# The order of the seven products, and of their loads, in the tokens-stationary groups of a hybrid decoder trunk

## The chip, the core and the metric

The kernel runs on one core of one Trainium2 chip. A core has five engines with a queue each: TensorE (PE in the profile; its weight loads are listed apart as PEld), VectorE (DVE), ScalarE (ACT), GpSimd (POOL) and SyncE (SP). SP and POOL also issue DMA transfers between the chip's main memory and SBUF. TensorE writes into PSUM, of which this kernel uses eight banks of 128 × 512 float32; VectorE and ScalarE read them out. The metric is the device time of one execution in microseconds (us), as a median over runs, lower is better.

## The reference

Two layers of a decoder trunk on 512 tokens of width 1024, all in float32. Each layer has one wide input projection that feeds a dilated-window attention and a chunked retention, two projections that are merged by sigmoid gates, an output projection and a SwiGLU feed-forward part. What matters here is the input projection:

```python
z = jnp.einsum('bsd,dc->bsc', x, w_in) + b_in
q_a, k_a, v_a, q_r, k_r, v_r, g_r, gate_a, gate_b = jnp.split(z, SPLIT_POINTS, axis=-1)
...
y_r = _retention(q_r, k_r, v_r)                       # reshapes left out
y_b = (jax.nn.silu(g_r) * y_r.reshape(B, S, RET_V_WIDTH)).astype(x.dtype)
```

`v_a` (the attention's values, 1152 columns), `v_r` and `g_r` (the retention's values and its gate, 2048 columns each, in four heads of 512) are the columns that the changed groups compute.

## The kernel before

**Precision.** Each float32 matrix is split into a high and a low part (`hi` is a cast by ScalarE, `lo` a subtraction by VectorE), and a product is the sum of three matmuls: high × high, high × low and low × high.

**Seven products in place of eight.** A group computes a 2 × 2 block product. The left side is x transposed, cut into token halves and halves of the depth: A11, A12, A21, A22, and four sums of them, S1 to S4, that are made once per sublayer (tiles `xh`, `xl` for the blocks, `xs` for the sums). The right side is a block of weights, B11, B12, B21, B22: the first index is the half of the depth, the second is one of two column ranges. Four sums of weights stand beside them: P1, P2, P3 and P4. The seven products are M1 = A11·B11, M2 = A12·B21, M3 = S4·B22, M4 = A22·P4, M5 = S1·P1, M6 = S2·P2 and M7 = S3·P3. Three chains accumulate in PSUM (`CHAIN`, L296): chain A takes M1, M6, M7 and M4 on top of each other and is read out in between after each of them, chain X is M2 alone, and chain C takes M5 and then M3.

**Two kinds of groups.** In a *tokens-stationary* group (`tall`, L372) x is loaded into the PE array and the weights stream by; each product is done for two token tiles (`a` = 0, 1), 24 matmuls in all, and has two PSUM banks per chain. In a *wide* group (`wide`, L393) the weights are loaded into the array and x streams. The tokens-stationary groups are, per layer: two groups of 288 columns for the attention's values (the loop over `t` that calls `biased`; one bias row enters as an extra matmul from tile `bh` before each half of M1 and M5), and four groups of 512 columns, one per retention head (`ret_values_gates`). That makes 12 groups in two layers. Each head's group follows that head's `rotary`, the projection of its queries and keys; between the matmuls, `tick` feeds in *side work* from a list, such as score blocks of the retention, at a set pace.

**The weights of a group** (class `Right`, L301). `load` issues, name by name and in two units of half the depth each, a DMA from SP into a `raw` tile (pool `rawp`, eight tiles for the whole kernel). For P1 and P3 the tile first takes one block (B11 or B12) and then a second DMA, issued by POOL, adds another block to it in flight (L316, B12 or B22). P2 is made from P1 by a VectorE addition of B22 in place (L342), P4 from P2 by an addition of B21. `high` casts a unit on ScalarE (`whi`, L325), `low` subtracts on VectorE (`wlo`, L331); `whi` and `wlo` have four tiles each, so the units of two products. `operands` (L345) casts one product ahead. A raw tile comes free when its last cast and subtraction (or addition) is done, and the next load, often that of the next group, takes it.

**Read-outs** (`ev` in `biased`, L451). After M1, M5 and M6 ScalarE copies the bank to a work tile (`sn`, L453; the pool `wk` has six tiles). After M2 VectorE adds it to the copy of M1; after M7 it subtracts from the copy of M5 (L460); the result for M3 is subtracted from with the copy of M6 (L457); M4 is read directly. The value groups write the results to main memory (`v_d`) by SP's DMAs (L762).

**What sets the order.** The code is a straight line; a tile library makes the semaphores and, before the run, chooses the order of each queue, which need not be that of the code. Products are written in the order of the tuple `ORDER` (L294): M1, M2, M5, M3, M6, M7, M4. As M3 comes before M6 there and its read-out needs M6's copy, `tall` does that read-out after M6. Loads are written in the order B11, B21, P1, P3, B22.

Of the kernel before, what the change touches and what calls it, by code (L numbers as in the profile page):

```python
# [18 lines left out]
P = 128  # L19
# [34 lines left out]
def hybrid_kernel(ctx, tc, x, rel_bias, w_in, b_in, w_attn_proj, w_ret_proj, w_out,  # L54
# [25 lines left out]
    def mm(ps, a, b, start, stop):  # L80
        pe.matmul(ps, lhsT=a, rhs=b, start=start, stop=stop, skip_group_check=True)  # L81

    def mm3(ps, ah, al, bh, bl, start, stop):
        mm(ps, ah, bh, start, False)
        mm(ps, ah, bl, False, False)
        mm(ps, al, bh, False, stop)

    def psum(name="px"):
        return psm.tile([P, S], F32, tag="mm", name=name)

    def hilo(src, hi, lo):
        act.copy(out=hi, in_=src)  # L92
        dve.tensor_tensor(out=lo, in0=src, in1=hi.bitcast(F32), op=ALU.subtract)  # L93
# [4 lines left out]
    def work(name):  # L98
        return wk.tile([P, S], F32, tag="w2", name=name)

    def rows(w):
        return w.rearrange("(k p) c -> p k c", p=P)
# [30 lines left out]
    def tick(us):  # L133

        if side:
            credit[0] += rate[0] * us
            while side and credit[0] >= 1.0:
                credit[0] -= 1.0
                side.popleft()()
# [138 lines left out]
    def tail_units(raws):  # L278

        out_ = []  # L280
        for j, r in enumerate(raws):
# [12 lines left out]
    ORDER = ((1, "A11", "B11"), (2, "A12", "B21"), (5, "S1", "P1"), (3, "S4", "B22"),  # L294
             (6, "S2", "P2"), (7, "S3", "P3"), (4, "A22", "P4"))
    CHAIN = {1: "A", 6: "A", 7: "A", 4: "A", 2: "X", 5: "C", 3: "C"}  # L296
    FIRST = (1, 2, 5)
    WIDE = tuple(ORDER[i] for i in (0, 2, 4, 1, 5, 3, 6))
    WIDE1 = tuple(ORDER[i] for i in (0, 1, 2, 4, 3, 5, 6))

    class Right:  # L301

        def __init__(self, src, shapes, order=ORDER, loads=("B11", "B21", "P1", "P3", "B22")):
            self.src, self.shapes, self.order, self.loads, self.t = src, shapes, order, loads, {}

        def load(self, *names):
# [41 lines left out]
                ahead = self.begin(self.order[i + 1][2]) if i + 1 < len(self.order) else None  # L351
                yield now

    def pair_right(w1, w2, c, order=WIDE):

        def src(b, u):
            k = 4 if b[1] == "2" else 0
            return (w2 if b[2] == "2" else w1)[:, k:k + 4, c:c + 256]

        return Right(src, [(4, 256)], order, ("B11", "P1", "B22", "P3", "B21"))  # L360
# [11 lines left out]
    def tall(right, n, left, ev, bias_=None):  # L372


        ps = {}
        for (i, an, bn), units in zip(ORDER, right.operands()):
            ks = [(u, k) for u in units for k in range(u[0].shape[1])]
            c = CHAIN[i]
            for a in range(2):
                fresh = i in FIRST  # L380
                if fresh:
                    ps[c, a] = psum("ps")[:, :n]
                if bias_ is not None and i in (1, 5):
                    mm(ps[c, a], ones, bias_[:, (i != 1) * n:(i != 1) * n + n], True, False)
                    fresh = False
                ts_ = slice(a * P, (a + 1) * P)
                for j, ((h, l), k) in enumerate(ks):
                    p_ = ps[c, a]
                    ah, al = left(an, j, ts_)
                    mm(p_, ah, h[:, k], fresh and j == 0, False)  # L390
                    mm(p_, ah, l[:, k], False, False)
                    mm(p_, al, h[:, k], False, j == len(ks) - 1)
                    tick(STEP * n / 512)  # L393
                if i != 3:
                    ev(i, a, ps[c, a])
                if i == 6:
                    ev(3, a, ps["C", a])
            yield

    def wide(right, left, ev):  # L400


        ps = {}
        for (i, an, bn), ((h, l),) in zip(right.order, right.operands()):
            c = CHAIN[i]
            if i in FIRST:
                ps[c] = psum("ps")
            for q in range(2):
                cs = slice(q * P, (q + 1) * P)
                for k in range(4):  # L410
                    ah, al = left(an, k, slice(0, 256))
                    mm3(ps[c][:, q * 256:(q + 1) * 256], h[:, k, cs], l[:, k, cs], ah, al,
                        i in FIRST and q == 0 and k == 0, k == 3)
                    tick(STEP / 2)
            ev(i, ps[c])
# [29 lines left out]
    def biased(right, n, rows_, left, right_done):  # L445


        sn = {}

        def ev(i, a, ps):  # L450
            if i in (1, 5, 6):  # L451
                sn[i, a] = work("sn")[:, :n]
                act.copy(out=sn[i, a], in_=ps)  # L453
            elif i == 2:
                left(a, ps, sn[1, a])
            elif i == 3:
                dve.tensor_tensor(out=sn[6, a], in0=ps, in1=sn[6, a], op=ALU.subtract)  # L457
                right_done(a, sn[6, a])
            elif i == 7:
                dve.tensor_tensor(out=sn[5, a], in0=sn[5, a], in1=ps, op=ALU.subtract)  # L460
                right_done(2 + a, sn[5, a])
            elif i == 4:
                left(2 + a, ps, None)

        return tall(right, n, x_left, ev, rows_)
# [158 lines left out]
    def layer(ly, cp):  # L624
# [197 lines left out]
        with stage("ret") as rp:  # L822
# [85 lines left out]
            def gates(dp, sa, sb):  # L908

                sn = {}  # L910

                def put(o_, v, c, ts_):
                    for q in range(2):
                        act.activation(out=o_[:, q, ts_], in_=v[:, q], func=AF.Sigmoid, bias=bcol(c + (2 * dp + q) * P))

                def ev(i, ps):
                    p2 = ps.rearrange("p (q t) -> p q t", q=2)
                    if i in (1, 5, 6):
                        sn[i] = work("sn").rearrange("p (q t) -> p q t", q=2)
                        act.copy(out=sn[i], in_=p2)  # L920
                    elif i == 2:
                        dve.tensor_tensor(out=sn[1], in0=p2, in1=sn[1], op=ALU.add)
                        put(sa, sn[1], C_GA, slice(0, 256))
                    elif i == 3:
                        dve.tensor_tensor(out=sn[6], in0=p2, in1=sn[6], op=ALU.subtract)
                        put(sb, sn[6], C_GB, slice(0, 256))
                    elif i == 7:
                        dve.tensor_tensor(out=sn[5], in0=sn[5], in1=p2, op=ALU.subtract)
                        put(sb, sn[5], C_GB, slice(256, 512))
                    elif i == 4:  # L930
                        put(sa, p2, C_GA, slice(256, 512))

                wide(pair_right(w_l[:, :, C_GA:], w_l[:, :, C_GB:], dp * 256), x_left, ev)
                act.dma_start(g_d[1, dp * 256:(dp + 1) * 256].rearrange("(e p) s -> p e s", p=P), sb)
# [17 lines left out]
            for dp in range(KD // 2):  # L952
# [6 lines left out]
                for e in range(2):  # L959
                    cs = slice(e * P, (e + 1) * P)  # L960
                    ps = psum("ps")
# [93 lines left out]
        wg_l, wu_l, wd_l = rows(w_ffn_gate[ly]), rows(w_ffn_up[ly]), rows(w_ffn_down[ly])  # L1055
# [16 lines left out]
        def ffn_pair(f, o_):  # L1072

            sn = {}

            def put(v, ts_):
                hilo(v, o_[:, 0, :, ts_], o_[:, 1, :, ts_])

            def ev(i, ps):
                p2 = ps.rearrange("p (q t) -> p q t", q=2)  # L1080
                if i in (1, 5, 6):
                    sn[i] = work("sn").rearrange("p (q t) -> p q t", q=2)
                    act.copy(out=sn[i], in_=p2)
                elif i == 2:
                    dve.tensor_tensor(out=sn[1], in0=p2, in1=sn[1], op=ALU.add)
                elif i == 3:
                    v = sn[6]
                    dve.tensor_tensor(out=v, in0=p2, in1=v, op=ALU.subtract)
                    act.activation(out=v, in_=v, func=AF.Silu)
                    dve.tensor_tensor(out=v, in0=v, in1=sn[1], op=ALU.mult)  # L1090
                    put(v, slice(0, 256))
                elif i == 7:
                    dve.tensor_tensor(out=sn[5], in0=sn[5], in1=p2, op=ALU.subtract)
                    act.activation(out=sn[5], in_=sn[5], func=AF.Silu)
                elif i == 4:
                    v = sn[5]
                    dve.tensor_tensor(out=v, in0=v, in1=p2, op=ALU.mult)
                    put(v, slice(256, 512))

            wide(pair_right(wu_l, wg_l, f * P, WIDE1 if f == 2 else WIDE), x_left, ev)  # L1100

        for part, (f0, f1) in enumerate(FPARTS):
            ht = []
# [89 lines left out]
```

## Time and profile before

| | us |
|---|---|
| median of 3 runs | 2190.7 |
| lowest, highest | 2188.38, 2191.09 |
| the profiled execution | 2188.09 |
| its span in the profile | 2186.3 |

The profile is that of one execution. Its span goes from the first instruction to the last and is 1.8 us shorter than the time of that execution; the rest lies around it. The page gives for each engine the time in which it was busy. Views of the trace that are used below: the *waits* (who waited for whom, in total), the *timeline* (instructions in order of time; in brackets the idle time before one and what ended it), the *windows* (busy time of each engine in a stretch), and the *DMA* view (transfers by the line that issues them, with the time to landing). Matmuls are pipelined, so their lengths overlap; the distance between two starts tells the pace.

### The profile page before, as it was taken

How to read it: one execution, taken by the hardware profiler on the slowest of the kernel's cores; microseconds unless marked ns; L12 is line 12 of the kernel's file. 1: busy time of each engine (PE TensorE's matmuls, PEld its weight loads, DVE VectorE, ACT ScalarE, POOL GpSimd, SP SyncE). 2: the span in 40 equal slices, each digit the busy share in tenths (PEclk: the TensorE clock that was granted, in tenths of full speed). 3: DMA queues.
4: the chain of work that ended last, by engine and by line, in shares of the span. 5: the costliest groups of instructions: out<-in, count | busy, mean ns of one | idle time of the engine just before them, and what ended most of it. 6: DMA issues, size and time to landing. Idle time of an engine off the chain costs nothing.

```text
span 2186.3 us, 32588 instructions
## 1 busy us (share of the span) xinstructions
PE 2160.0 (99%) x12906; PEld 1900.6 (87%) x12906; DVE 1412.5 (65%) x2035; ACT 988.1 (45%) x1597; POOL 254.1 (12%) x296
## 2 busy tenths in 40 slices
PE   8999999999999999999999999999999999999998
PEld 7977888889988899989898778888899889999996
DVE  5643677877655685747676446777777447766575
ACT  4444544545733263525245445445566233444350
POOL 3110011011000100000030100111110001000001
PEclk9999999999999999999999999999999999999999
DMA  8944266458685356656369342665577762666561
GB/s 228 244 125 104 58 165 159 132 136 192 192 307 189 91 150 133 172 134 156 95 158 260 90 92 74 152 180 144 137 191 223 267 194 58 172 150 165 123 163 39
DMA packets 305978, 338.60 MB, mean 155 GB/s; under 512 B 22862, under 2 KB 244194, under 8 KB 305697
## 3 DMA queue, kind: packets, MB, share of 16 engines
q1 hardware_dynamic: 227712, 248.81, 37.8%
q0 software_dynamic: 50832, 74.90, 18.2%
q10 hardware_dynamic: 27280, 12.80, 2.0%
q8 instruction: 101, 1.65, 0.3%
q14 instruction: 53, 0.43, 0.1%
HBM read 310.67 MB, written 28.53 MB: 155 GB/s over the span
## 4 chain that ended last, share of the span: by engine, by line
PE 82%; issue 9%; DMA 3%; DVE 3%; ACT 1%; POOL 1%; POOLq 0%; DVEq 0%; ACTq 0%; SPq 0%
PE ps L81 75%; PE px L81 5%; DMA raw<-in_w_in 2%; PE px L865 1%; PE px L533 1%; POOL ry L124 0%; DMA exd<-wb 0%; DVE wlo L331 0%; PE px L169 0%; DMA exd<-pk 0%; DVE wlo L93 0%; DVE xtok L988 0%; DMA mb<-exd 0%; DMA rb<-in_b_in 0%; ACT whi L92 0%
## 5 line engine op out<-in xcount | busy, mean ns | idle before, releaser
L331 DVE TENSOR_TENSOR wlo<-raw,whi 128x1024 fp32r<-128x1024 f32 (+1 forms) x364 | 418.1, 1150 | 210.0 <-ACT whi L325 207.3
L81 PE MATMUL ps<-xh,whi 128*128 128x256 f32 (+1 forms) x1536 | 515.7, 337 | 4.4 <-ACT whi L92 3.3
L325 ACT CAST whi<-raw 128x1024 fp32r<-128x1024 f32 (+1 forms) x364 | 358.8, 990 | 342.1 <-PE ps L81 198.5
L81 PE MATMUL ps<-xh,wlo 128*128 128x256 f32 (+1 forms) x1536 | 500.5, 327 | 1.1 <-DVE wlo L93 0.9
L81 PE MATMUL ps<-xl,whi 128*128 128x256 f32 (+1 forms) x1536 | 500.5, 326 | 0.2 <-DVE xl L93 0.2
L81 PE MATMUL ps<-xs,whi 128*128 128x256 f32 (+1 forms) x2048 | 404.6, 296 | 0.0
L81 PEld LDWEIGHTS ps<-xs,whi 128*128 128x128 f32 x2048 | 327.8, 191 | 10.3
L93 DVE TENSOR_TENSOR wlo<-raw,whi 128x1024 fp32r<-128x1024 f32 (+2 forms) x162 | 193.3, 1195 | 200.9 <-ACT whi L92 200.5
L81 PEld LDWEIGHTS ps<-xh,whi 128*128 128x128 f32 x1536 | 292.1, 191 | 33.6 <-issue 6.4
L81 PEld LDWEIGHTS ps<-xh,wlo 128*128 128x128 f32 x1536 | 292.5, 191 | 26.3 <-DVE wlo L93 1.5
L81 PEld LDWEIGHTS ps<-xl,whi 128*128 128x128 f32 x1536 | 293.5, 191 | 19.2 <-DVE xl L93 1.0
L81 PE MATMUL ps<-xs,wlo 128*128 128x256 f32 (+1 forms) x1024 | 303.4, 296 | 0.0
L92 ACT CAST whi<-raw 128x1024 fp32r<-128x1024 f32 (+2 forms) x162 | 165.2, 1028 | 235.1 <-PE ps L81 151.6
L81 PE MATMUL ps<-whi,xs 128*128 128x512 f32 (+1 forms) x768 | 219.9, 360 | 1.8 <-ACT whi L325 1.3
L81 PEld LDWEIGHTS ps<-xs,wlo 128*128 128x128 f32 x1024 | 196.0, 191 | 5.0
L81 PE MATMUL ps<-whi,ht 128*128 128x512 f32 x576 | 178.4, 389 | 0.0
L81 PEld LDWEIGHTS ps<-whi,xs 128*128 128x128 f32 x768 | 137.6, 188 | 22.5 <-ACT whi L325 1.8
L81 PE MATMUL ps<-wlo,xs 128*128 128x512 f32 (+1 forms) x384 | 138.1, 360 | 1.2 <-DVE wlo L331 1.2
L316 POOL DMA_DIRECT2D raw<-in_w_ffn_gate x40 | 51.7, 1293 | 680.3 <-DMA raw<-in_w_ffn_up 312.3
L81 PEld LDWEIGHTS ps<-whi,ht 128*128 128x128 f32 x576 | 108.1, 188 | 22.3
L316 POOL DMA_DIRECT2D raw<-in_w_in x64 | 80.3, 1273 | 358.2 <-DMA raw<-in_w_in 160.8
L342 DVE TENSOR_TENSOR raw<-raw 128x1024 f32<-128x1024 f32 (+1 forms) x104 | 119.5, 1149 | 2.1
(185 smaller groups left out, 2951.7 us busy)
## 6 DMA issues: line engine op xcount, KB each, us to landing
raw<-in_w_in SPq DMA_DIRECT2D x152, 512.0 KB, 4.2
raw<-in_w_ffn_up SPq DMA_DIRECT2D x64, 512.0 KB, 4.1
raw<-in_w_in POOLq DMA_DIRECT2D x48, 512.0 KB, 8.3
raw<-in_w_ffn_gate SPq DMA_DIRECT2D x44, 512.0 KB, 4.8
raw<-in_w_ffn_down SPq DMA_DIRECT2D x44, 512.0 KB, 4.1
raw<-in_w_ffn_gate POOLq DMA_DIRECT2D x40, 512.0 KB, 6.5
raw<-in_w_in SPq DMA_DIRECT2D x72, 256.0 KB, 5.3
raw<-in_w_ret_proj SPq DMA_DIRECT2D x32, 512.0 KB, 6.3
```

Source lines behind the costliest of these rows:

```text
L81: pe.matmul(ps, lhsT=a, rhs=b, start=start, stop=stop, skip_group_check=True)
L92: act.copy(out=hi, in_=src)
L93: dve.tensor_tensor(out=lo, in0=src, in1=hi.bitcast(F32), op=ALU.subtract)
L316: pool.dma_start(r, self.src({"P1": "B12", "P3": "B22"}[n], u), accum_op=ALU.add)
L325: act.copy(out=h, in_=src)
L331: dve.tensor_tensor(out=l, in0=src, in1=h.bitcast(F32), op=ALU.subtract)
L342: dve.tensor_tensor(out=r, in0=r, in1=self.t["B22" if n == "P2" else "B21", u], op=ALU.add)
L533: pe.transpose(px[:, (2 + j) * P:(3 + j) * P], s[:, hh, j * P:(j + 1) * P], ident)
L865: pe.transpose(px[:, t * P:(t + 1) * P], ys[i][:, t * P:(t + 1) * P], ident)
```

## The change

The tokens-stationary groups take their products in the order M1, M5, M6, M2, M7, M3, M4, which `wide` had been using under the name `WIDE`; `Right` uses it by default, and loads by default in the order B11, P3, P1, B22, B21. M3 now comes after M6, and the read-out of M3 moves to its own place. `pair_right` still passes its own loads and keeps them; the two orders of the wide groups get new names with the same content.

```diff
@@ -295,15 +295,15 @@
     CHAIN = {1: "A", 6: "A", 7: "A", 4: "A", 2: "X", 5: "C", 3: "C"}
     FIRST = (1, 2, 5)
-    WIDE = tuple(ORDER[i] for i in (0, 2, 4, 1, 5, 3, 6))
-    WIDE1 = tuple(ORDER[i] for i in (0, 1, 2, 4, 3, 5, 6))
+    SPACED = tuple(ORDER[i] for i in (0, 2, 4, 1, 5, 3, 6))
+    SUMS2 = tuple(ORDER[i] for i in (0, 1, 2, 4, 3, 5, 6))
...
-        def __init__(self, src, shapes, order=ORDER, loads=("B11", "B21", "P1", "P3", "B22")):
+        def __init__(self, src, shapes, order=SPACED, loads=("B11", "P3", "P1", "B22", "B21")):
...
-    def pair_right(w1, w2, c, order=WIDE):
+    def pair_right(w1, w2, c, order=SPACED):
...
-        for (i, an, bn), units in zip(ORDER, right.operands()):
+        for (i, an, bn), units in zip(right.order, right.operands()):
...
-                if i != 3:
-                    ev(i, a, ps[c, a])
-                if i == 6:
-                    ev(3, a, ps["C", a])
+                ev(i, a, ps[c, a])
...
-            wide(pair_right(wu_l, wg_l, f * P, WIDE1 if f == 2 else WIDE), x_left, ev)
+            wide(pair_right(wu_l, wg_l, f * P, SUMS2 if f == 2 else SPACED), x_left, ev)
```

## The prediction

> **What bounds the kernel now.** I read the page first, then the PE rows of the view of waits, then the timelines of the stages that the change touches.
>
> ```profile
> span 2186.3 us, 32588 instructions
> PE 2160.0 (99%) x12906; PEld 1900.6 (87%) x12906; DVE 1412.5 (65%) x2035; ACT 988.1 (45%) x1597; POOL 254.1 (12%) x296
> ```
>
> TensorE is busy 99% of the span, so time is won only where PE stands still, and every new PE stall is paid in full: nothing behind it has slack to take it up. The view of PE's waits says how little there is to win:
>
> ```profile
> PE ps L81 <- DVE sn L460: 2.4, 4, 1.1
> PE ps L81 <- ACT whi L325: 1.3, 2, 0.7
> PE ps L81 <- DVE wlo L331: 1.2, 3, 0.4
> PE ps L81 <- ACT sn L453: 0.3, 1, 0.3
> ```
>
> Columns: who waited for whom, us in total, times, longest. The two `sn` rows are what this order of products costs: a product adds into the PSUM bank that the product just before it filled, so it waits until that bank was read out. The timelines place them, all in head 0 (these are layer 0's; layer 1 has the other two):
>
> ```profile
> 262.12 0.50 PE L81 MATMUL ps<-whi,xs 128*128 128x512 f32 x1 [0.33 <-ACT sn L453]
> ...
> 282.87 0.47 PE L81 MATMUL ps<-whi,xh 128*128 128x512 f32 x1 [1.06 <-DVE sn L460]
> ...
> 286.81 0.50 PE L81 MATMUL ps<-whi,xh 128*128 128x512 f32 x1 [0.24 <-DVE sn L460]
> ```
>
> The `whi L325` and `wlo L331` rows are waits for weights. They sit in the attention-value groups (288 columns, two per layer); the windows show which, one row per group, layer 0 and then layer 1:
>
> ```profile
> 52.90:75.90 23.00, 23.00 (x173) 22.88 (x173) 16.13 (x26) 12.36 (x22) 6.43 (x9) 1.00 0.84 211
> 75.90:101.20 25.30, 23.88 (x175) 23.20 (x174) 16.32 (x24) 12.85 (x23) 3.69 (x3) 1.00 1.03 260
> 1135.10:1158.00 22.90, 22.90 (x173) 22.87 (x172) 16.24 (x26) 12.39 (x22) 5.07 (x7) 1.00 0.76 180
> 1158.00:1182.60 24.60, 23.55 (x175) 23.11 (x174) 16.31 (x24) 12.79 (x23) 3.60 (x3) 1.00 0.99 250
> ```
>
> Stretch, its length, PE busy, and at the end of the row clock, DMA share and GB/s. The first group of a layer runs dense (23.0 and 22.9 us); the second takes 2.3 and 1.7 us more, at a DMA share of 1.03 and 0.99. These groups are DMA-limited, and what they lack is P1, a sum made by two transfers: SP loads B11, then POOL adds B12 in flight.
>
> **The change, part by part.** It touches 12 groups: per layer two value groups (288 columns) and four heads (512 columns). Matmuls, casts, subtractions and DMAs stay the same in number; only orders move. The renamed orders of the `wide` groups are the same tuples, and these groups pass their own loads: nothing there.
>
> *Order of products, bank waits.* M1, M5, M6, M2, M7, M3, M4 puts a product of another chain between any two of one chain (A: M1, M6, M7, M4; C: M5, M3). The bank is then read out under a product that doesn't need it, so the five waits go: 2.4 + 0.3 = **2.7 us gained**. Next late there is only the weight cast, which is one product ahead. Bounds: 0, if DVE's backlog in head 0 only moves, and 3.2: the matmul after such a wait takes 0.47 to 0.50 us where a 512-column one otherwise takes 0.39 (the row of 320.80 below), 0.1 more at five places.
>
> *Order of products, P1.* M5 moves from third to second place and needs P1 one product earlier, and M2, which covered that time, comes later. In heads 1 to 3 P1 is there long before:
>
> ```profile
> 304.40 1.20 POOL L316 DMA_DIRECT2D raw<-in_w_in  x1 [4.50 <-ACT yt L867]
> ...
> 320.80 0.39 PE L81 MATMUL ps<-bh,ones 128*128 128x512 f32 x1
> ...
> raw<-in_w_in POOLq DMA_DIRECT2D x4, 288.0 KB, 7.8
> ```
>
> The last of head 1's four adds is issued at 304.40 and M1 starts at 320.80: 16.4 us, against 7.8 us to landing in the value groups, for tiles 1.8 times as large here (estimate 14). M5 has a whole M1 on top of that. I cost heads at nothing; if that cover went, a head would lose up to one product. In value groups there is no such room. The groups start with M1 where their windows above do (75.90, 1135.10, 1158.00). Here are the starts of M1 and of M5 in the very first group, and the casts of P1's second unit in all four (column one: start, column two: length; in brackets the idle time before and what ended it):
>
> ```profile
> 52.95 0.29 PE L81 MATMUL ps<-bh,ones 128*128 128x288 f32 x1
> ...
> 59.60 0.29 PE L81 MATMUL ps<-bh,ones 128*128 128x288 f32 x1
> ...
> 58.08 0.67 ACT L325 CAST whi<-raw 128x576 fp32r<-128x576 f32 x1 [1.08 <-DMA raw<-in_w_in]
> ...
> 84.28 1.82 ACT L325 CAST whi<-raw 128x576 fp32r<-128x576 f32 x3 [1.41 <-DMA raw<-in_w_in]
> 84.99 0.76 DVE L331 TENSOR_TENSOR wlo<-raw,whi 128x576 fp32r<-128x576 f32 x1 [0.83 <-ACT whi L325]
> ...
> 1139.26 0.67 ACT L325 CAST whi<-raw 128x576 fp32r<-128x576 f32 x1
> ...
> 1165.72 1.82 ACT L325 CAST whi<-raw 128x576 fp32r<-128x576 f32 x3 [2.18 <-DMA raw<-in_w_in]
> ```
>
> Between 52.95 and 59.60 lie M1 (24 matmuls and 2 bias rows) and M2 (24): 6.65 / 50 = 0.133 us each. M1 and M5 take 26 each, 3.46 us; M2 takes 3.19. After P1's second unit is cast (0.67) and subtracted (0.76), M5 still has 6 + 13 = 19 matmuls to do, 2.53 us. So M5 ends at cast + 3.96. With P1 landing when it does today:
> - layer 0, first: 58.08 + 3.96 = 62.04; without a wait 52.95 + 6.92 = 59.87. Loss 2.2.
> - layer 1, first: 1139.26 + 3.96 = 1143.22 against 1135.10 + 6.92 = 1142.02. Loss 1.2.
> - layer 0, second: 84.28 + 3.96 − 75.90 = 12.34 against 6.92: a wait of 5.4, of which 2.3 are paid already. Loss 3.1.
> - layer 1, second: 1165.72 + 3.96 − 1158.00 = 11.68: a wait of 4.75, 1.7 paid already. Loss 3.05.
>
> Sum **9.55 us lost**. While M5 waits, everything on PE waits behind it; on ACT M1's read-out stands behind the cast of P1, and nobody needs it before M6. P2 follows from P1 by an add, a cast and a subtraction (0.76 + 0.67 + 0.76 = 2.2 us), inside the 2.53 us that M5 has left: no second stall.
>
> *Order of loads.* P3's two loads and two POOL adds now stand before P1's, and B21's loads go last, into B11's freed tiles, where B22's were, needed by the fourth product as B22 was: no loss. P3 ahead of P1 cuts both ways:
>
> ```profile
> 74.48 1.28 POOL L316 DMA_DIRECT2D raw<-in_w_in  x1 [10.33 <-DVE sn L460]
> 76.95 3.69 POOL L316 DMA_DIRECT2D raw<-in_w_in  x3 [1.19 <-DVE wlo L331]
> ```
>
> POOL's four adds cost it 1.2 to 1.3 us each. Two of them before P1's can delay P1 by up to 2.5 us where POOL is the limit. But P1 keeps its sixth and seventh place among SP's loads, and POOL has been idle 10 us before the first add; P3's adds can be out before P1's first load lands, and then cost only bandwidth. Earlier: the last loads of a group wait for raw tiles of the group before, and there P3 is now used fifth, not sixth, which frees two tiles one product (3.2 us) sooner. I take zero, between +2.5 and −3.2. With +2.5 at each of the four places the loss is 19.55; with −3.2 it is 0 (no group can lose less than its own M5 wait).
>
> *Work tiles.* The read-outs of M1, M5 and M6 now come before M2's sum frees any, so six tiles of the six-tile work pool are held for one product. Side work that wants one in that time would wait. In value groups there is none; in heads 1 to 3 the score blocks begin after eight empty slots, in the fifth product. I cost it at nothing, bound 1 us per head.
>
> **Sum**: 9.55 − 2.7 = +6.85 us on the profiled execution's 2188.09 us, 2194.9. The median of the runs is 2190.7, 2.6 above that execution, so against it: **2197.5 us**, 0.3% slower. A measurement of this kernel can tell about 0.2%, 4.4 us, from no change.
>
> **The rivals.**
> 1. *P1 comes sooner, a wash.* Freed tiles and the early adds bring P1 about 3 us forward; the second groups lose nothing more and the first ones little, say 2.2 in layer 0. For it: POOL idle 10.33 us before its first add. Against it: in second groups DMA is at a share of 1.0, so what goes earlier displaces something. 2190.7 + 2.2 − 2.7 = 2190.2.
> 2. *The other side, faster.* The same mechanism, larger: P1's second unit in the second groups must be cast by 3.46 + 0.93 − 1.43 = 2.96 us after M1's start (0.93: the first unit's seven matmuls). Today it is 84.28 − 75.90 = 8.38. From 5.4 us sooner on, today's waits of 2.3 and 1.7 go too: 2190.7 − 4.0 − 2.7 = 2184.0. Freed tiles give 3.2 at most, so it needs much of the queue emptied besides.
> 3. *The clock falls.* PE idles long enough in the new waits for the throttle to halve the clock. The trace has one such case, after PE sat idle 3.3 us for ACT at the start:
>
> ```profile
> 9.00:12.00 3.00, 0.27 (x2) 0.27 (x3) 1.64 (x4) 3.00 (x7) 0.00 (x0) 1.00 1.09 346
> 12.00:15.00 3.00, 2.86 (x17) 2.65 (x17) 2.37 (x5) 1.24 (x3) 0.00 (x0) 0.68 1.10 341
> 15.00:18.00 3.00, 3.00 (x21) 3.00 (x21) 0.62 (x1) 1.05 (x1) 0.00 (x0) 0.75 1.14 308
> ```
>
>    The granted clock fell to 0.68 and 0.75: (0.32 + 0.25) × 3 = 1.7 us lost. The new waits are 5.4, 4.75, 2.2 and 1.2 us, each cut in two by seven matmuls. If three of them trip it: 2197.5 + 5.1 = 2202.6. The Trainium skill, page "TensorE: Matmul & The Clock Gate", section "HAM oscillation — how this bites in real kernels", has PE-idle gaps over about 3.4 us as what lowers the clock. By it the split waits, each piece near or under 3.3 us, would mostly go free and 2197.5 would stand; the row above, idle for 3.3 and yet slowed, speaks for the rival.
> 4. *The change doesn't reach the queues.* The order of a queue is not that of the code, as SP's rows show:
>
> ```profile
> 63.00 0.32 SPq L790 DMA_DIRECT2D v<-v_d  x1
> 63.42 0.38 SPq L109 DMA_DIRECT2D raw<-in_w_in  x1
> ```
>
>    Here a load of `v`, written after both value groups in the code, goes out ahead of the second group's loads. If M2 stayed ahead of M5 on PE, 2190.7. Against it: B21 is now loaded last, so M2 can't be ready first.
>
> **How the numbers follow.** Forecast 0.42, clock 0.20, wash 0.22, no effect 0.04, faster 0.12. Slower by over 0.2% (above 2195.1): 0.42 + 0.20 = 0.62. Within: 0.26. Faster: 0.12. The range goes from 2187.0, under the wash with its gain, to 2206.5, just under the loss with every add delayed (2190.7 + 19.55 − 2.7 = 2207.55); it leaves out most of the faster case and the worst of the clock's.
>
> **What would show it.** The `sn L460` and `sn L453` rows of PE's waits are gone. The value groups' windows read about 25, 28.5, 24 and 27.5 us, with M5, now second, waiting for `whi L325` and `wlo L331`, and POOL's third and fourth adds, no longer the first two, released by P1's loads. Heads 1 to 3 keep their length. Wrong would be: value groups no longer than today (P1 early), a granted clock under 1.00 in them (rival 3), or new PE waits in heads 1 to 3 for a work tile or a bank.

## The result, and the profile after

| | before | changed |
|---|---|---|
| median of 6 runs, us | 2191.03 | 2206.73 |
| lowest, highest | 2188.38, 2195.12 | 2204.68, 2211.08 |
| span of the profiled execution | 2186.3 | 2202.9 |

The changed kernel takes 1.0073 times as long (95% interval 1.0062 to 1.0084), 15.7 us more. The forecast, 2197.5 us, had the sign right and the size less than half: 6.8 us over the median it was made from. The time lies just above the range given.

The head of the changed kernel's page, and its PE rows of the view of waits (who waited for whom: us in total, times, longest):

```profile
span 2202.9 us, 32603 instructions
...
PE 2168.2 (98%) x12906; PEld 1908.1 (87%) x12906; DVE 1413.6 (64%) x2035; ACT 990.4 (45%) x1597; POOL 253.7 (12%) x296
```

```profile
PE ps L81 <- ACT whi L325: 12.5, 5, 5.8
...
PE ps L81 <- DVE wlo L331: 2.1, 8, 0.4
```

The number of matmuls is the same, and PE is busy 8 us longer with them, mostly a matter of the clock, as will be seen. The two `sn` rows of before are gone, and the waits for `whi` and `wlo` have gone from 2.5 to 14.6 us. The windows of the four value groups (length first; then busy time of PE, PEld, DVE, ACT, POOL; at the end granted clock, DMA share, GB/s):

```profile
52.70:81.60 28.90, 26.69 (x173) 25.65 (x173) 17.26 (x27) 12.19 (x22) 9.03 (x14) 0.88 0.70 180
81.60:113.90 32.30, 26.13 (x174) 24.91 (x173) 16.33 (x24) 13.19 (x23) 0.70 (x1) 0.89 0.81 214
1145.80:1171.40 25.60, 24.14 (x173) 23.09 (x173) 16.99 (x27) 12.19 (x22) 5.06 (x7) 1.00 0.59 141
1171.40:1202.60 31.20, 26.14 (x173) 24.91 (x172) 16.32 (x24) 13.14 (x23) 2.37 (x2) 0.89 0.86 232
```

Together 118.0 us, where the same four rows of before add up to 95.8: the groups lose **22.2 us**. Of the eight heads two got shorter, the first one of each layer. Before and then changed, its row for layer 0 and for layer 1:

```profile
243.70:320.80 77.10, 75.47 (x349) 61.61 (x349) 58.00 (x98) 36.74 (x55) 11.42 (x15) 1.00 0.55 141
1325.30:1402.40 77.10, 75.65 (x349) 61.56 (x349) 56.77 (x97) 36.04 (x53) 11.29 (x15) 1.00 0.56 139
```

```profile
256.70:331.50 74.80, 74.78 (x348) 61.82 (x348) 58.30 (x99) 36.83 (x55) 11.36 (x15) 1.00 0.55 145
1344.00:1418.60 74.60, 74.58 (x348) 61.89 (x348) 58.21 (x99) 36.61 (x55) 11.26 (x15) 1.00 0.56 145
```

They gain 2.3 and 2.5 us, **4.8** in all, and PE now stands still for 0.02 us in each. 22.2 − 4.8 = 17.4, against 16.6 by the two spans; the other 0.8 is scatter of stretches that the change does not touch. So two things happened, a gain in the heads and a loss nearly five times as large in the value groups, and the first question is why P1 is so late there. The second value group of layer 0 shows it, on PE (start, length, in brackets the idle time before and what ended it), and then on ACT:

```profile
85.08 0.29 PE L81 MATMUL ps<-bh,ones 128*128 128x288 f32 x1
91.16 0.61 PE L81 MATMUL ps<-whi,xs 128*128 128x288 f32 x1 [5.79 <-ACT whi L325]
91.95 0.61 PE L81 MATMUL ps<-wlo,xs 128*128 128x288 f32 x1 [0.18 <-DVE wlo L331]
```

```profile
90.44 0.67 ACT L325 CAST whi<-raw 128x576 fp32r<-128x576 f32 x1 [9.82 <-DMA raw<-in_w_in]
...
92.81 0.67 ACT L325 CAST whi<-raw 128x576 fp32r<-128x576 f32 x1 [1.40 <-DMA raw<-in_w_in]
```

M5 begins at 85.08 with its bias row and stands for 5.79 us, until ACT has cast P1's first unit, and ACT had been idle 9.82 us for that unit's DMA. The second unit is cast at 92.81, which is 11.2 us after the group's start (81.60). Before, it was 84.28 − 75.90 = 8.4. P1 did not land when it used to; it came 2.8 us later. The summary of POOL's adds (L316) around this group, before and then changed, says where that comes from (duration in ns; first and last start; then the time from issue to landing):

```profile
L316 POOL DMA_DIRECT2D raw<-in_w_in x4: 1212/1415/1701, 74.5 to 79.1; - x4
...
DMA to landing us min/median/max: 7.3/7.8/8.5
```

```profile
L316 POOL DMA_DIRECT2D raw<-in_w_in x4: 1214/1484/1794, 75.7 to 80.5; - x4
...
DMA to landing us min/median/max: 7.3/10.1/12.2
```

In the changed kernel P1's second unit is the last of the four, issued at 80.5, so 1.1 us ahead of the group's start. Before, it was the second of the four, issued at 76.95 (its row stands in the prediction), 1.05 us after the start. It is thus issued 2.15 us *earlier* and lands later, because the time to landing has gone from 7.3 (the first two adds of before) to 12.2. In this group P1 did not lose a turn on POOL; its add, now the last of four, is longer on its way. It is not alone in that: SP's own loads issued beside it (77.0 to 81.1) took 6.2 to 12.0 us to land, against 5.2 to 6.1 for those before (71.0 to 76.3).

The other groups are not all like this one. ACT's casts of P1's second unit in the first group of layer 0 and in the two of layer 1 (those of before stand in the prediction):

```profile
59.12 0.67 ACT L325 CAST whi<-raw 128x576 fp32r<-128x576 f32 x1 [2.04 <-DMA raw<-in_w_in]
...
1151.03 0.67 ACT L325 CAST whi<-raw 128x576 fp32r<-128x576 f32 x1 [1.61 <-DMA raw<-in_w_in]
...
1181.49 0.67 ACT L325 CAST whi<-raw 128x576 fp32r<-128x576 f32 x1 [1.54 <-DMA raw<-in_w_in]
```

With the traces' times of the adds, for P1's second unit, before → changed (us; issue and cast are counted from the group's start):

| group | add issued | time to landing | cast |
|---|---|---|---|
| layer 0, first | −3.4 → −4.1 | 8.5 → 10.4 | 5.2 → 6.4 |
| layer 0, second | 1.05 → −1.1 | 7.3 → 12.2 | 8.4 → 11.2 |
| layer 1, first | −4.9 → −1.8 | 8.9 → 6.9 | 4.2 → 5.2 |
| layer 1, second | 0.1 → 1.3 | 7.6 → 8.7 | 7.7 → 10.1 |

P1 is later in all four, by 1.2, 2.8, 1.1 and 2.4 us, 7.5 in all. In layer 0 the add is issued earlier and takes longer; in layer 1 it is issued 3.1 and 1.2 us later, so there the delay begins before the add.

### The profile page after: what moved, and what is told of

Same layout as the page of the kernel before. It is cut to its first block, busy times and chain, and to the rows that moved or that the text cites. A ratio compares the mean times of both kernels' runs of the same rounds, so it can differ in the third digit from the quotient of the medians.

```text
span 2202.9 us, 32603 instructions
## 1 busy us (share of the span) xinstructions
PE 2168.2 (98%) x12906; PEld 1908.1 (87%) x12906; DVE 1413.6 (64%) x2035; ACT 990.4 (45%) x1597; POOL 253.7 (12%) x296
## 4 chain that ended last, share of the span: by engine, by line
PE 87%; issue 5%; DMA 4%; DVE 2%; ACT 1%; POOL 1%; SPq 0%; POOLq 0%; DVEq 0%; ACTq 0%
PE ps L81 78%; PE px L81 7%; DMA raw<-in_w_in 3%; PE px L530 1%; PE px L862 1%; POOL ry L124 0%; DMA exd<-wb 0%; PE px L169 0%; DVE xtok L985 0%; DMA exd<-pk 0%; DVE wlo L331 0%; DVE wlo L93 0%; DMA mb<-exd 0%; PE px L586 0%; DVE xc L185 0%
## 5 line engine op out<-in xcount | busy, mean ns | idle before, releaser
L81 PE MATMUL ps<-whi,xs 128*128 128x512 f32 (+1 forms) x768 | 227.5, 367 | 12.7 <-ACT whi L325 12.5
L81 PEld LDWEIGHTS ps<-whi,xs 128*128 128x128 f32 x768 | 142.8, 195 | 34.1 <-ACT whi L325 14.6
L316 POOL DMA_DIRECT2D raw<-in_w_ffn_gate x40 | 51.8, 1294 | 681.9 <-DMA raw<-in_w_ffn_up 313.1
L316 POOL DMA_DIRECT2D raw<-in_w_in x64 | 80.1, 1297 | 316.4 <-DMA raw<-in_w_in 173.3
```

Source lines behind the costliest of these rows:

```text
L316: pool.dma_start(r, self.src({"P1": "B12", "P3": "B22"}[n], u), accum_op=ALU.add)
```

## The experiments

Beside each stands the median of the kernel before on the same chip; the ratio is to that. In all of them `biased` gives `Right` an order and loads by the width of the group (`VB`, 288, the value groups), and where the old order `ORDER` is used, M3's read-out stands after M6 as it did:

```diff
-        return Right(src, [(k, n) for k in nk])
+        order, loads = VALUES if n == VB else HEADS
+        return Right(src, [(k, n) for k in nk], order, loads)
...
-                ev(i, a, ps[c, a])
+                if i != 3 or right.order is not ORDER:
+                    ev(i, a, ps[c, a])
+                if i == 6 and right.order is ORDER:
+                    ev(3, a, ps["C", a])
```

`VALUES` and `HEADS` stand here for the pairs that each experiment writes out. "Old" is `ORDER` with B11, B21, P1, P3, B22, "new" is `SPACED` with B11, P3, P1, B22, B21.

**Heads alone and value groups alone.**

```diff
# e1_heads
+ VALUES = old      HEADS = new
# e2_values
+ VALUES = new      HEADS = old
```

> The new order of products and of loads in the eight head groups (512 columns) alone; the four value groups (288 columns) as before. Theory (the whole loss comes from the value groups, where P1 is late and the clock falls): the waits of the kernel before for a bank in head 0 (2.4 + 0.3 us) are gone, nothing new appears, 2 to 3 us under the kernel before. Rival (the heads lose too, for a work tile, a bank or P1): above the kernel before, with new PE waits between 245 and 505 us.

> The new orders in the four value groups alone; the heads as before. Theory: the changed kernel's loss plus the 2.7 us that the heads won, 17 to 20 us over the kernel before, with the clock halved three times between 50 and 1190 us. Rival (heads lose): clearly less than the changed kernel's loss of 16 us.

Before: 2189.07 us. e1_heads: 2184.8, ratio 0.9979 (0.9969 to 0.9988), 4.3 us faster. e2_values: 2210.59, ratio 1.0098 (1.0083 to 1.0113), 21.5 us slower. The heads gained more and the value groups lost more than was expected, and in the profile of e2_values the clock halves in all four groups, not in three. The two add up to +17.2, about what the changed kernel loses (15.7 here, 13.1 when it ran again as e9_changed). So the orders are good for the heads and bad for the value groups, and the loss has to be looked for in the latter alone. One caution for the windows: the value groups of e1_heads are those of before, and in its profiled execution they come to 98.1 us instead of 95.8 (by the starts of their matmuls). A sum of four windows scatters by some 2 us; part of it here is a fall of the clock in layer 0's second group, from 88.47 to 91.89, which the profile of before does not have.

**Which of the two orders.** The next pair takes the two changes apart. e3_p1_first keeps the new products in the value groups and loads P1 before P3. e4_p3_ahead is the kernel before but for one exchange in the value groups' loads, P3 ahead of P1.

```diff
# e3_p1_first
+ VALUES = SPACED, ("B11", "P1", "P3", "B22", "B21")      HEADS = new
# e4_p3_ahead
+ VALUES = ORDER, ("B11", "B21", "P3", "P1", "B22")       HEADS = old
```

> The changed kernel, but the value groups load P1 ahead of P3 (B11, P1, P3, B22, B21). Theory as it now stands: P3 ahead of P1 makes P1 land about 3 us later in each of the second groups and 1 to 3 us later in the first ones; with P1 first about 8 us of PE waits and part of the clock's loss go, leaving 3 to 8 us over the kernel before. Rival (the order of products alone makes the loss; transfers are slow because the queue is full, whichever goes first): within 3 us of the changed kernel, 13 us or more over the kernel before.

> The kernel before in everything but the value groups' loads: P3 ahead of P1 (B11, B21, P3, P1, B22), products in the old order with M5 third. Theory (P3 ahead delays P1 by about 3 us in second groups): today's waits of 2.3 and 1.7 us there grow to about 5 us each, 5 to 8 us over the kernel before, more if the clock falls. Rival (P3's adds go out early and cost nothing): within 2 us of the kernel before.

e3_p1_first: 2184.23, ratio 0.9975 (0.9964 to 0.9986), 4.8 us **faster** than before: the expectation missed by nearly 8 us at the least. e4_p3_ahead: 2203.66, ratio 1.0063 (1.0048 to 1.0078), 14.6 us slower with the old order of products: twice what was expected without a fall of the clock. The windows of the four value groups, e3_p1_first and then e4_p3_ahead (columns as above):

```profile
52.60:77.60 25.00, 23.46 (x173) 22.96 (x173) 16.16 (x26) 11.63 (x21) 8.14 (x13) 1.00 0.75 191
77.60:102.80 25.20, 23.67 (x174) 22.97 (x173) 15.98 (x24) 12.98 (x23) 1.86 (x2) 1.00 0.97 260
1133.10:1156.00 22.90, 22.90 (x173) 22.90 (x172) 15.92 (x25) 11.74 (x21) 6.71 (x9) 1.00 0.67 173
1156.00:1180.20 24.20, 23.40 (x174) 22.95 (x173) 15.98 (x24) 13.08 (x23) 0.72 (x1) 1.00 0.93 245
```

```profile
52.50:80.50 28.00, 25.23 (x173) 24.40 (x173) 16.14 (x26) 12.09 (x22) 6.64 (x9) 0.94 0.70 177
80.50:110.50 30.00, 25.32 (x174) 24.71 (x173) 16.32 (x24) 12.59 (x23) 3.69 (x3) 0.89 0.90 227
1143.20:1168.50 25.30, 24.34 (x174) 23.15 (x174) 16.06 (x26) 11.95 (x22) 5.07 (x7) 1.00 0.66 164
1168.50:1198.60 30.10, 26.13 (x174) 25.41 (x173) 16.35 (x24) 12.62 (x23) 3.60 (x3) 0.89 0.91 232
```

97.3 and 113.4 us. ACT's casts of P1 in the second group of layer 0 tell why, again e3_p1_first first (its group starts at 77.60, that of e4_p3_ahead at 80.50):

```profile
78.00 0.67 ACT L327 CAST whi<-raw 128x576 fp32r<-128x576 f32 x1 [1.38 <-DMA raw<-in_w_in]
82.57 0.67 ACT L327 CAST whi<-raw 128x576 fp32r<-128x576 f32 x1 [3.60 <-DMA raw<-in_w_in]
```

```profile
91.23 0.67 ACT L327 CAST whi<-raw 128x576 fp32r<-128x576 f32 x1 [8.39 <-DMA raw<-in_w_in]
92.74 1.82 ACT L327 CAST whi<-raw 128x576 fp32r<-128x576 f32 x3 [0.54 <-DVE wlo L333]
```

With P1 ahead its second unit is cast 5.0 us after the group's start, with P3 ahead 12.2 us after it. Each of the two kernels differs from another one by nothing in the value groups but the exchange of these two names: e4_p3_ahead is 3.8 us later than before (8.4), e3_p1_first 6.2 us sooner than the changed kernel (11.2). The exchange moves P1 at more than one point of its way. In the second group of layer 0, with P3 ahead, P1's second add is issued 3.0 us after the start in e4_p3_ahead, 2.0 later than before, and takes 9.2 us to land, 1.9 longer; in e3_p1_first it is issued 2.6 us sooner than in the changed kernel and takes 8.6 us, 3.6 less. What the two exchanges show is that P1's place in the list makes the loss; how much of it is SP's order, POOL's order or what else is in flight, they do not separate. The order of products, which was to cost 9.55 us in the value groups, costs next to nothing against the kernel before when P1 is the first sum to be loaded, which is sooner than it was there: of e3_p1_first's 4.8 us gained, the heads explain 4.3.

**A version that beats both.** If the order of loads is what counts, the old order of products, which needs P1 third, should like P1 loaded second, with the heads in the new orders.

```diff
# e6_p1_second
+ VALUES = ORDER, ("B11", "P1", "B21", "P3", "B22")       HEADS = new
```

> Heads with the new orders, value groups with the old order of products and P1 loaded second (B11, P1, B21, P3, B22). Theory: the heads' 2.7 us are won, and P1 comes early enough to take part of the second groups' 4.0 us of waits; B21, now behind P1's base loads, is needed one product after M1 and may wait instead by 1 to 2 us. 3 to 6 us under the kernel before. Rival (B21 takes over P1's wait): no better than the run with the heads alone.

Before: 2188.63. e6_p1_second: 2179.49, ratio 0.9958 (0.9944 to 0.9973), 9.1 us faster than before, more than the 3 to 6 expected, and by the two ratios 1.1% faster than the changed kernel. Its four windows:

```profile
53.00:76.00 23.00, 23.00 (x175) 22.96 (x174) 16.15 (x26) 12.35 (x22) 8.11 (x10) 1.00 0.90 233
76.00:99.40 23.40, 23.35 (x174) 22.94 (x173) 16.08 (x24) 12.43 (x23) 2.39 (x2) 1.00 0.94 236
1128.70:1151.60 22.90, 22.90 (x173) 22.87 (x172) 16.15 (x26) 12.30 (x22) 6.94 (x9) 1.00 0.68 165
1151.60:1175.10 23.50, 23.45 (x174) 23.03 (x173) 16.07 (x24) 12.58 (x23) 2.37 (x2) 1.00 0.97 238
```

PE is busy in every one of them for all but 0.05 us, 92.8 us in all. No wait is left even in the second groups, which had been called DMA-limited at shares of 1.03 and 0.99. That does not yet show that bandwidth was to spare: the groups load the same weights, but by length times GB/s their windows move 5.5 and 5.6 MB here, against 6.6 and 6.2 MB before, so some of the moving now falls outside of them. The next kernel tells more.

**What P3's adds in flight cost.** A rival had it that P1 suffers from P3's transfers beside it, not from its place. Then B22 between the two should help.

```diff
# e8_p1_b22
+ VALUES = SPACED, ("B11", "P1", "B22", "P3", "B21")      HEADS = new
```

> The changed kernel, with the value groups' loads in the order B11, P1, B22, P3, B21, so that P3's adds go out after P1's and after B22. Theory (what is issued ahead of P1, in POOL's queue and among the loads, decides when it lands; with P1 second the second unit lands 4 to 5 us after the start of M1 in second groups whatever comes after): waits like those of the run with B11, P1, P3, about 5 us in the four groups, 3 to 6 us under the kernel before; P3, fifth, stays in time. Rival (P3's adds, in flight together with P1's, slow them): 2 us or more faster than with B11, P1, P3, near the best run so far, 9 us under the kernel before.

Before: 2188.77. e8_p1_b22: 2181.97, ratio 0.9971 (0.9962 to 0.998), against 0.9975 (0.9964 to 0.9986) for e3_p1_first: no difference that can be told. Its value groups take 23.0, 24.5, 22.9 and 23.4 us, 93.8 in all, which is 3.5 less than those of e3_p1_first, in one profile each and with a scatter of 2. The 6.8 us gained lie between the two expectations. Whether P3's transfers slow P1's a little stays open; it is small beside P1's place in the list.

The row of its last group answers the question of bandwidth:

```profile
1152.60:1176.00 23.40, 23.12 (x174) 22.89 (x173) 16.16 (x24) 13.11 (x23) 2.37 (x2) 1.00 1.02 274
```

At a DMA share of 1.02 it moves 6.4 MB in 23.4 us, and PE stands still for 0.28 us. The same group of before took 24.6 us for 6.2 MB at a share of 0.99. A share near 1.0 thus did not set the length of the group; what counted was which of the transfers came first.

**How much of the loss is the clock.** The rows of the changed kernel show clocks of 0.88 and 0.89. Two experiments keep PE at work in the waits with extra matmuls, into a PSUM bank of their own that nobody reads; what the kernel computes is the same.

```diff
# e5_fill: fills = deque((5, 34, 0, 28)); e7_fill_both: deque((6, 36, 2, 30))
+            if i == 1 and fills and n == VB:          # after M1
+                pd = psum("fill")[:, :n]
+                for _ in range(fills.popleft()):
+                    mm(pd, ah, h[:, k], True, True)
# e7_fill_both alone, after the first unit of M5
+                    if n == VB and i == 5 and a == 0 and j == 1:
+                        pd = psum("fill")[:, :n]
+                        for _ in range(8):
+                            mm(pd, ah, h[:, k], True, True)
```

> The changed kernel with extra matmuls of 288 columns after M1 in the value groups (5, 34, 0 and 28 of them at 0.133 us, in the order of the groups), into a PSUM bank that nobody reads; they fill the time in which M5 waits for P1, and change nothing else. Theory (the clock's fall costs time of its own): the two falls in the second groups go, P1 lands as before; 3 to 4 us less than the changed kernel, 6 if the first group's fall goes too. Rival (the fall only accompanies the wait and the work after it is bound by P1 anyway): within 1 us of the changed kernel, or more where the extra matmuls overrun the wait.

e5_fill: 2202.51, ratio 1.0061 (1.0042 to 1.0081) on a chip where before took 2188.63. It tells little: the changed kernel did not run beside it, and the profile of e5_fill still has two falls of the clock, both in layer 1, one of them in the group that got no extra matmuls. The waits before M5's second unit were not filled anywhere. So e7_fill_both fills both waits in all four groups, and e9_changed is the changed kernel once more, on the same chip.

> The changed kernel with both parts of M5's wait for P1 filled in all value groups: 6, 36, 2 and 30 extra matmuls after M1 and 8 after M5's first unit in each group, into banks that nobody reads. In the run with 5, 34, 0 and 28 the matmuls at half pace fell from 5.4 us to 3.7 us, since two falls of the clock were left in layer 1. Theory (the fall costs its half-paced matmuls): no fall left between 50 and 1200 us, waits and extra matmuls together as long as the changed kernel's waits of 21 us, 4 to 6 us less than the changed kernel on the same chip. Rival (P1 binds, a faster pace only waits longer): within 1.5 us of the changed kernel.

> The changed kernel once more, on the chip of the next two runs: 13 to 18 us over the kernel before, half clock after each of three of the four value groups' waits. It is the base for the run with the filled waits.

Before: 2188.77. e9_changed: 2201.87, ratio 1.0064 (1.005 to 1.0078). e7_fill_both: 2197.59, ratio 1.0044 (1.0031 to 1.0056), 4.3 us less than e9_changed though it does 106 matmuls more. Their value groups, e9_changed and then e7_fill_both:

```profile
53.80:81.40 27.60, 25.33 (x174) 24.33 (x173) 17.26 (x27) 12.20 (x22) 9.90 (x14) 0.94 0.72 190
81.40:113.90 32.50, 27.28 (x173) 26.05 (x173) 16.33 (x24) 13.16 (x23) 0.00 (x0) 0.84 0.79 210
1143.50:1169.20 25.70, 24.04 (x174) 23.08 (x173) 17.00 (x27) 12.11 (x22) 5.14 (x8) 1.00 0.59 144
1169.20:1200.50 31.30, 26.20 (x173) 25.15 (x173) 16.33 (x24) 13.20 (x23) 2.31 (x2) 0.89 0.83 225
```

```profile
53.50:80.40 26.90, 25.79 (x187) 24.90 (x187) 17.00 (x27) 12.02 (x22) 8.58 (x13) 1.00 0.70 175
80.40:110.00 29.60, 29.22 (x218) 28.75 (x217) 16.15 (x24) 13.07 (x23) 1.20 (x1) 1.00 0.84 224
1141.20:1166.50 25.30, 24.88 (x184) 24.39 (x184) 17.00 (x27) 12.22 (x22) 5.20 (x8) 1.00 0.59 146
1166.50:1196.90 30.40, 28.68 (x211) 28.00 (x211) 16.15 (x24) 13.12 (x23) 2.23 (x2) 1.00 0.84 225
```

The clock is 1.00 throughout, and the groups take 112.2 us instead of 117.1. The stretches without useful work have not become shorter: by the starts of the matmuls the waits of e9_changed are 19.9 us long, and those of e7_fill_both 5.5, which with 14.1 us of extra matmuls (106 at 0.133 us) is 19.6. P1's second units land at nearly the same times, counted from the groups' starts (0.4 us less in the sum of the four). Idle waits turned into work that is thrown away are worth 4.9 us in the groups and 4.3 in the time: that is what the clock took of the loss. The rest is P1's lateness, and filling does nothing against it.

## Why the prediction was off, step by step

**Order of loads, taken as zero: the step that failed.** It set the loads between −3.2 and +2.5 us a place and took nothing, on the ground that P3's adds "can be out before P1's first load lands, and then cost only bandwidth". P3's adds did go out ahead, and that cost more than bandwidth: P1's second unit came 1.2, 2.8, 1.1 and 2.4 us later in the four places, 7.5 us where the sum has nothing. The bound of +2.5 a place was near the truth; the zero was not. The reason given for it looked at POOL's turn alone, where the bound of 2 × 1.25 us comes from, and not at the whole way of the transfer. In layer 0 POOL did issue P1 sooner than before (by 0.7 and 2.15 us), but the adds land in the order in which they are issued, in the second group P1's two 2.4 us apart (casts at 90.44 and 92.81, both released by DMA), and P1's took 2.0 and 5.0 us longer. In layer 1 P1's own add went out 3.1 and 1.2 us later. Why the one happens here and the other there stays open; that P1's place in the list makes the delay is shown by the two exchanges, 3.8 and 6.2 us in layer 0's second group. In the kernel before, where P1 falls from the third place to the fourth, the exchange alone costs 14.6 us (e4_p3_ahead), the half clock in it included.

**Order of products, P1, 9.55 us.** The arithmetic (M5 ends at the cast of P1's second unit + 3.96) was sound, and with the landing of before the sum may be right; that was not tried. Its premise was wrong, that P1's landing is given. From the starts of the matmuls, PE's waits in the four groups went from 3.5 to 21.0 us, 17.5 instead of 9.55 more. The 8 us between are the loads: P1's casts alone are 7.5 us later. With P1 loaded first the same order of products costs at most a few us (e3_p1_first against e6_p1_second: 0.9975 to 0.9958, intervals that touch).

**The clock, rival 3, 5.1 us at a chance of 0.20.** It came true, and at its price. That the price fits is in part luck: it was made from a fall of 3.4 us. The clock halves three times in the value groups of the changed kernel, for 6.8 us each, twice that long, but PE waits in part of that time; from the pace of the matmuls that costs 5.0 us more than before, and e7_fill_both gets 4.3 back. What was misjudged is the chance, as the waits themselves were taken too short: "each piece near or under 3.3 us" turned out as 5.79 in layer 0's second group. With the forecast's 2197.5 the clock's 5.1 gives 2202.6, and the 8 us of waits take it to 2210.6, less the 2 that the heads brought beyond their term in these profiles: 2208.5, against 2206.73 measured.

Two of the falls follow a standstill of over 3.4 us, 5.79 in layer 0's second group and some 4.5 in layer 1's, and here the rule that was cited from the Trainium skill, page "TensorE: Matmul & The Clock Gate", section "HAM oscillation — how this bites in real kernels" (gaps over about 3.4 us), and the trace agree. The other one, the first in time, does not fit it. The first value group of the changed kernel, in windows of 3.4 us, and then PE's waits in it by the timeline:

```profile
52.56:55.97 3.41, 3.41 (x27) 3.37 (x26) 0.00 (x0) 0.00 (x0) 1.32 (x3) 1.00 1.14 245
55.97:59.39 3.42, 1.85 (x10) 1.17 (x9) 2.18 (x3) 0.94 (x2) 1.06 (x2) 1.00 1.12 312
59.39:62.80 3.41, 2.77 (x10) 2.45 (x11) 2.91 (x5) 2.64 (x6) 0.00 (x0) 0.50 0.32 100
62.80:66.20 3.40, 3.40 (x16) 3.40 (x16) 2.22 (x4) 1.51 (x3) 0.58 (x1) 0.50 0.00 0
```

```profile
57.13 0.40 PE L81 MATMUL ps<-whi,xs 128*128 128x288 f32 x1 [0.65 <-ACT whi L325]
57.92 0.40 PE L81 MATMUL ps<-wlo,xs 128*128 128x288 f32 x1 [0.40 <-DVE wlo L331]
...
59.84 0.61 PE L81 MATMUL ps<-whi,xs 128*128 128x288 f32 x1 [0.98 <-ACT whi L325]
```

The row of the second stretch counts 10 matmuls, two of which had begun before it; the other 8 are 1.1 us of work at 0.133 us each. The longest wait in or beside it was 0.98 us; the next two stretches ran at 0.50. By the rule this group would have kept its clock.

The traces show what tells these cases apart. In all eleven profiles the changes of the clock lie on a grid of 3.41 us, that of the windows above. In the value groups sixteen stretches of this grid at full clock hold ten starts of their 288-column matmuls or fewer, and the clock is halved after every one of them; the thinnest stretch after which it stayed at 1.00 holds eleven (e5_fill). A dense one holds some 25. So here it was the thinness of a whole stretch that counted, not one long wait, and a wait of less than 3.4 us costs clock or not by where it falls on the grid. Even the old orders can be caught: e1_heads, whose value groups are those of before, was caught with 8 starts and no wait above 0.87 us. Its stretch and the one after it, and then the thinnest stretch that kept the clock, of e5_fill:

```profile
85.06:88.47 3.41, 1.93 (x10) 1.25 (x10) 2.34 (x4) 1.79 (x4) 0.00 (x0) 1.00 1.20 207
88.47:91.89 3.42, 3.42 (x16) 3.42 (x16) 2.47 (x5) 0.96 (x3) 0.00 (x0) 0.50 0.61 155
```

```profile
59.25:62.67 3.42, 1.95 (x13) 1.50 (x12) 2.80 (x5) 2.12 (x5) 0.00 (x0) 1.00 0.40 127
```

**Bank waits, −2.7 us.** Right in kind: both `sn` rows are gone, and e1_heads shows the gain by itself. The size is less sure than the kind. From the start of head 0 to that of head 1, both layers together, the changed kernel takes 149.4 us; of the three profiles with the old orders in the heads, e2_values takes 152.0, e4_p3_ahead 152.8 and before 154.1. So the gain is 2.6, 3.4 or 4.7 us by profile, and the 4.3 of e1_heads has an interval from 2.6 to 6.8: the bound of 3.2 may have been too low, but this does not show it. In the rows of head 0 above, PE's idle time falls by 3.0 us (1.63 and 1.45 to 0.02 each), and its busy time by 1.8 besides (75.47 to 74.78 and 75.65 to 74.58); why the latter falls was not examined.

**Heads at nothing, work tiles at nothing.** Right: no wait of PE for a work tile, a bank or a P1 shows in the heads.

**The wash and the faster rival.** Both rested on P1 coming sooner. The changed kernel gave the contrary. The loads in another order bear the mechanism out in part: with the old order of products no wait is left (e6_p1_second), with the new one e8_p1_b22 comes nearest, P1 there some 4 us sooner than before in the second groups and 1.2 and 0.28 us of idle PE left in them. That the price of 2184.0 is close to e3_p1_first's 2184.23 is luck. The price was 6.7 us under its base, the run won 4.8 under its own, 2189.07, and of these 4.3 are the heads'; its second groups still take 25.2 and 24.2 us, hardly less than before. **That the change doesn't reach the queues** fell: M5 is second on PE.

**Windows of 25, 28.5, 24 and 27.5 us** came out as 28.9, 32.3, 25.6 and 31.2: each 1.6 to 3.9 longer, in all four.

## What to carry to other kernels

Before a list of loads is reordered, number the transfers of each DMA queue and see which place the one has that is used first: in the second group of layer 0 an issue 2.15 us earlier did not help P1, which stood behind P3 and landed 2.8 us later. When an order of products and an order of loads change together, price the loads first, and try the new product order with its operand loaded first; here the exchange of two names turned 0.7% of loss into 0.25% of gain (e3_p1_first). And a wait on PE can cost more than its length: where it left ten matmul starts or fewer in a stretch of 3.41 us, what followed ran at half the clock, and filling such waits with matmuls that nobody reads won 4.3 us.

## What the runs showed of the hardware

- Adds in flight of 288 KB that POOL issued for a value group landed in the order of issue in all eleven profiles. With four close together, time to landing rose from 7.3 us for the first to 12.2 us for the last (changed kernel). SP's loads beside them took up to 12.0 us as well, so the rise is not shown to be that queue's alone.
- A DMA share near 1.0 over a group did not mean that bandwidth set its length: layer 1's second group took 24.6 us for 6.2 MB at a share of 0.99 before, and 23.4 us for 6.4 MB at 1.02 in e8_p1_b22, with 0.28 us of idle PE.
- The granted clock changed on a grid of 3.41 us. In the value groups it was halved after each stretch at full clock with ten starts of 288-column matmuls or fewer (sixteen stretches, one with no wait above 0.87 us) and stayed after each with eleven or more, where a dense stretch has some 25. A half-clock time lasted one, two or three stretches there.
